# Modulation sets on VectorE: from column sweeps over a 128 x 512 accumulator to fused row sums over transposed blocks, in a hybrid encoder block

## The chip, the cores and the metric

The kernel runs on one core of a Trainium2 chip. Its time is device microseconds of one execution. A measurement is the median of several executions; for the kernel before it is 1263.94 us over three runs (1263.31 to 1264.48).

The names in the text: TensorE (PE in the profile) multiplies matrices, VectorE (DVE) does elementwise work and sums along the free dimension, ScalarE (ACT) applies functions and copies, SyncE (SP) issues the loads and stores. PEld is TensorE's loading of the stationary operand.

## The reference

One layer of an encoder block over 256 tokens of width 2048, all in float32. A conditioning vector c (2048 numbers) makes six modulation vectors of 2048 numbers each:

```
c_act = silu(c)
mod = c_act @ ada_w + ada_b                       # 2048 x 12288
shift_a, scale_a, gate_a, shift_f, scale_f, gate_f = split(mod, 6)

h = rmsnorm(x, norm1_w) * (1 + scale_a) + shift_a
proj = h @ w_in                                   # 2048 x 5184
...
x = x + gate_a * (concat(ret_out, mla_out) @ w_o)
h = rmsnorm(x, norm2_w) * (1 + scale_f) + shift_f
x = x + gate_f * ((silu(h @ w_gate) * (h @ w_up)) @ w_down)
out = rmsnorm(x, final_norm_w)
```

Between the two lines with proj and x stand eight heads of bidirectional retention and eight heads of latent attention. The change touches only how mod is computed.

## The kernel before, in words

**Layout.** Features are cut into 16 tiles of 128 (K tiles). All weights come as one stream in the order in which they are used (class Stream), in loads of mostly 128 x 1024 floats, 512 KB, into six buffers named stg. A weight tile is split into a rounded part whi (ScalarE, line 124) and a remainder wlo (VectorE, line 126), and each product takes three matmuls (lines 132 to 134): high by high, high by low, low by high. The products accumulate in eight PSUM banks.

**Stages.** The input projection runs over four groups of K tiles (GROUPS: 2, 4, 4 and 6 tiles). For each group build_h1 (line 360) makes the scaled and shifted input from xnT, the column of gain_a and the column of mod, two ScalarE operations (lines 143 and 144, tiles hfull and actt) and a VectorE subtraction (line 145) for a tile. The scale and shift of a group are therefore needed before its matmuls; they are computed during the group before. After that come retention and attention, the output projection, the second norm, the gated feed-forward and the down projection.

**Modulation sets.** mod is computed in sets (ada_set, line 174): one section (SC_A and SH_A are scale and shift of the first norm, SC_F and SH_F of the second, GT_A and GT_F the gates) and up to four feature blocks of 128, so 512 columns of ada_w. A set is either TensorE's or VectorE's, by the strings ADA_PE, ADA_PE2 and ADA_PE3. A TensorE set multiplies each weight tile by a padded copy c_pad of silu(c) (line 196) into four rows of a bank. A VectorE set has the 2048 input features on the partitions and the 512 columns along the free dimension, and sweeps the 16 K tiles:

```
V.tensor_scalar(out=a, in0=w[:, j], scalar1=c_act[:, 0:1], scalar2=None, op0=ALU.mult)
V.scalar_tensor_tensor(out=a, in0=w[:, j], scalar=c_act[:, k:k + 1], in1=a, op0=ALU.mult, op1=ALU.add)
```

(lines 198 and 200). The accumulator ada_acc then holds 128 partial sums for each column. For scale and shift, spread() turns each of the set's blocks with a TensorE transpose (line 222), sums along the free dimension (line 226, VectorE) and adds the bias (line 227). For a gate, a matmul with a matrix of ones (line 218) sums over the partitions and spreads the result to all of them at once.

Sixteen sets are VectorE's. Thirteen of them run while the pool mid is open: SH_A of blocks 2 to 5; SC_A of blocks 6 to 9, 10 to 13 and 14 to 15 (the last with 256 columns); GT_A of blocks 0, 8 and 12; SC_F of 0 and 4; SH_F of 4 and 8; and SC_F and SH_F of 12. The other three, GT_F of blocks 4, 8 and 12, run later beside the feed-forward.

**Order.** The program lists steps (the list steps, from line 370 on) and mixes the loads of the sets among the weight loads. run() issues loads up to four tiles ahead of their use. A scheduler then decides, from its own estimates, in which order each engine gets its instructions; each engine then works through its list in order, with waits on semaphores.

Of the kernel before, what the change touches and what calls it, by code (L numbers as in the profile page):

```python
# [29 lines left out]
R_GA, R_GF, R_GNW, R_GNB, R_FW, R_RD, R_FREQ = 0, 2048, 4096, 5120, 6144, 8192, 8208  # L30
N_ROWS = 8304
# [30 lines left out]
class Stream:  # L62

    def __init__(self, ap):
        self.ap, self.at, self.plan = ap, 0, []

    def take(self, name, k0, kt, c0, n):
        self.plan.append((name, k0, kt, c0, n))  # L70
        a = self.at
        self.at += P * kt * n
        return self.ap[a:self.at].rearrange("(p f) -> p f", p=P)

    def pack(self, np, weights):
        flat = np.empty(self.at, np.float32)
        a = 0
        for name, k0, kt, c0, n in self.plan:
# [7 lines left out]
def encoder_block(ctx: ExitStack, tc: tile.TileContext, x, cols, rows, pos, stream, out):  # L86
# [8 lines left out]
    def bank():  # L95
        return ps.tile([P, 512], F32, name="bank")
# [14 lines left out]
    c_act = const.tile([P, KT], F32, name="c_act")  # L111
    c_pad = const.tile([P, KT, 32], F32, name="c_pad")
# [55 lines left out]
    def f(fn, *args):  # L168
        return ("f", lambda: fn(*args), fn.__name__)
# [4 lines left out]
    def ada_set(pool, sec, k0, nk, rowdst, on_pe):  # L174
        n = nk * P
        wide = n if not on_pe else min(n, 2 * P)
# [3 lines left out]
        def acc_tile():  # L180
            return (pool or late["pool"]).tile([P, n], F32, name="ada_acc", tag="ada_acc", bufs=2 if pool else 1, padded_shape=[P, 512])

        def load(c, t):
            w = wp.tile([P, kk, wide], F32, name="stg", tag="stg", bufs=6)
            SY.dma_start(w.rearrange("p k n -> p (k n)"), stream.take("ada_w", t * kk, kk, sec * D + k0 * P + c, wide))
            return w

        def body(c, t, w):
            if c == 0 and t == 0:
                acc["t"] = bank() if on_pe else acc_tile()  # L190
            a = acc["t"]
            for j in range(kk):
                k = t * kk + j
                if on_pe:
                    q = 32 * (k % 4)
                    PE.matmul(a[q:q + 32, c:c + wide], lhsT=c_pad[:, k], rhs=w[:, j], start=c == 0 and k < 4, stop=c + wide == n and k >= KT - 4)  # L196
                elif k == 0:
                    V.tensor_scalar(out=a, in0=w[:, j], scalar1=c_act[:, 0:1], scalar2=None, op0=ALU.mult)
                else:
                    V.scalar_tensor_tensor(out=a, in0=w[:, j], scalar=c_act[:, k:k + 1], in1=a, op0=ALU.mult, op1=ALU.add)  # L200

        def finish():
            a = acc["t"]
            if on_pe:
                b, a = a, acc_tile()
                S.copy(a, b[:, 0:n])
            acc["a"] = a
            if rowdst is not None:
                r0 = (R_GA if sec == GT_A else R_GF) + k0 * P
                br = wp.tile([1, n], F32, name="bias_row", tag="stg", bufs=6)  # L210
                SY.dma_start(br, rows[:, r0:r0 + n])
                V.tensor_tensor(a[0:1, :], a[0:1, :], br, op=ALU.add)

        def spread():
            a = acc["a"]
            b = bank()
            if rowdst is not None:
                PE.matmul(b[:, 0:n], lhsT=ones, rhs=a, start=True, stop=True)
# [6 lines left out]
            parts = b[:, 0:n].rearrange("p (j q) -> p j q", q=P)  # L225
            V.tensor_reduce(out=m, in_=parts[:, :, ::32] if on_pe else parts, axis=AX.X, op=ALU.add)  # L226
            V.tensor_tensor(m, m, col[:, C_ADAB + ks.start:C_ADAB + ks.stop], op=ALU.add)
# [24 lines left out]
    mid = mid_cm.__enter__()  # L252

# [4 lines left out]
    S.activation(c_act, col[:, C_C:C_C + KT], AF.Silu)  # L258
    G.memset(c_pad, 0.0)
    V.tensor_copy(c_pad[:, :, 0:1], c_act.unsqueeze(2))  # L260
# [112 lines left out]
    steps += [f(turn_x, 0), f(build_h1, 0)]  # L373
# [51 lines left out]
    krT = mid.tile([P, T], F32, name="krT")  # L425
# [293 lines left out]
    rstd_b = mid.tile([P, T], F32, name="rstd_b")  # L719
# [273 lines left out]
```

## Time and profile before

| | |
|---|---|
| median of three runs | 1263.94 us |
| profiled execution | 1266.85 us |
| its span, first to last instruction | 1264.9 us |
| TensorE busy | 1224.4 us, 97% |
| VectorE busy | 843.6 us, 67% |
| ScalarE busy | 599.7 us, 47% |
| mean granted TensorE clock | 0.992 |
| read from memory | 312.11 MB |

The profile is one execution. Its page gives each engine's busy time, the span cut into slices, the chain of waits that ended last (from the last instruction back to what released it, step by step) and the costliest groups of instructions. Matmuls overlap, so a matmul's own duration is longer than the step from one to the next, and the step is what counts. "Idle before" is the time an engine waited ahead of an instruction, with the one that released it.

### The profile page before, as it was taken

How to read it: one execution, taken by the hardware profiler on the slowest of the kernel's cores; microseconds unless marked ns; L12 is line 12 of the kernel's file. 1: busy time of each engine (PE TensorE's matmuls, PEld its weight loads, DVE VectorE, ACT ScalarE, POOL GpSimd, SP SyncE). 2: the span in 40 equal slices, each digit the busy share in tenths (PEclk: the TensorE clock that was granted, in tenths of full speed). 3: DMA queues.
4: the chain of work that ended last, by engine and by line, in shares of the span. 5: the costliest groups of instructions: out<-in, count | busy, mean ns of one | idle time of the engine just before them, and what ended most of it. 6: DMA issues, size and time to landing. Idle time of an engine off the chain costs nothing.

```text
span 1264.9 us, 16232 instructions
## 1 busy us (share of the span) xinstructions
PE 1224.4 (97%) x6022; PEld 971.6 (77%) x6022; DVE 843.6 (67%) x1185; ACT 599.7 (47%) x811; POOL 1.7 (0%) x9
## 2 busy tenths in 40 slices
PE   5899899999999999899999999999999999999997
PEld 2676667788787788578888888888888888888885
DVE  2596988879997998886655556655654454554544
ACT  4552454645556665646344444444444434444433
POOL 0000000000000000000000000000000000000000
PEclk9999999999999999999999999999999999999998
DMA  8888898888877887897667657665765655555552
GB/s 337 321 301 309 276 317 299 290 311 290 298 255 289 306 301 278 299 349 250 211 220 233 201 183 274 222 203 202 275 219 188 226 187 194 190 198 190 192 196 88
DMA packets 88799, 315.28 MB, mean 249 GB/s; under 512 B 10248, under 2 KB 10376, under 8 KB 88208
## 3 DMA queue, kind: packets, MB, share of 16 engines
q1 hardware_dynamic: 88720, 314.24, 72.0%
q8 instruction: 47, 0.77, 0.3%
q14 instruction: 32, 0.26, 0.1%
HBM read 312.11 MB, written 2.10 MB: 248 GB/s over the span
## 4 chain that ended last, share of the span: by engine, by line
PE 85%; DVE 5%; DMA 5%; ACT 2%; issue 1%; SPq 0%; ACTq 0%; DVEq 0%
PE bank L133 25%; PE bank L134 25%; PE bank L132 25%; DMA stg<-in_stream 5%; DVE wlo L126 2%; PE bank L148 2%; PE bank L196 2%; DVE ada_acc L200 1%; ACT whi L124 1%; PE bank L514 1%; PE bank L138 1%; PE bank L513 1%; PE bank L626 1%; PE bank L615 1%; PE bank L140 1%
## 5 line engine op out<-in xcount | busy, mean ns | idle before, releaser
L126 DVE TENSOR_TENSOR wlo<-stg,whi 128x1024 fp32r<-128x1024 f32 (+2 forms) x400 | 478.7, 1198 | 341.2 <-ACT whi L124 339.6
L124 ACT CAST whi<-stg 128x1024 fp32r<-128x1024 f32 (+2 forms) x400 | 412.8, 1033 | 532.3 <-PE bank L134 417.2
L132 PE MATMUL bank<-whi,actt 128*128 128x512 f32 (+1 forms) x1184 | 457.9, 393 | 11.7 <-ACT whi L124 8.4
L133 PE MATMUL bank<-wlo,actt 128*128 128x512 f32 (+1 forms) x1184 | 461.7, 390 | 7.4 <-DVE wlo L126 7.0
L134 PE MATMUL bank<-whi,actt 128*128 128x512 f32 (+1 forms) x1184 | 459.2, 388 | 0.3 <-DVE actt L145 0.3
L132 PEld LDWEIGHTS bank<-whi,actt 128*128 128x128 f32 x1184 | 222.0, 189 | 64.9 <-ACT whi L124 12.7
L133 PEld LDWEIGHTS bank<-wlo,actt 128*128 128x128 f32 x1184 | 223.7, 189 | 62.4 <-DVE wlo L126 17.0
L134 PEld LDWEIGHTS bank<-whi,actt 128*128 128x128 f32 x1184 | 223.7, 189 | 44.9 <-DVE actt L145 1.1
L200 DVE SCALAR_TENSOR_TENSOR ada_acc<-stg,c_act,ada_acc 128x512 f32<-128x512 f32 (+1 forms) x240 | 175.0, 730 | 15.8 <-DMA stg<-in_stream 12.8
L132 PE MATMUL bank<-whi,ap 128*128 128x512 f32 x352 | 137.0, 389 | 0.0
L134 PE MATMUL bank<-whi,ap 128*128 128x512 f32 x352 | 136.9, 389 | 0.0
L133 PE MATMUL bank<-wlo,ap 128*128 128x512 f32 x352 | 136.9, 389 | 0.0
L133 PEld LDWEIGHTS bank<-wlo,ap 128*128 128x128 f32 x352 | 66.1, 188 | 13.8
L132 PEld LDWEIGHTS bank<-whi,ap 128*128 128x128 f32 x352 | 66.1, 188 | 13.8
L134 PEld LDWEIGHTS bank<-whi,ap 128*128 128x128 f32 x352 | 66.1, 188 | 13.5
L196 PE MATMUL bank<-stg,c_pad 128*32 128x256 f32 x544 | 48.0, 415 | 11.1 <-DMA stg<-in_stream 11.0
L196 PEld LDWEIGHTS bank<-stg,c_pad 128*32 128x32 f32 x544 | 13.0, 112 | 35.2 <-issue 26.0
L852 ACT ACTIVATE sgs<-bank 128x512 f32<-128x512 f32 x22 | 13.1, 597 | 10.5 <-PE bank L134 9.8
L145 DVE TENSOR_TENSOR actt<-hfull,actt 128x256 fp32r<-128x256 f32 x40 | 16.3, 420 | 2.2 <-ACT actt L144 2.1
L854 DVE TENSOR_TENSOR sgs<-bank,sgs 128x512 f32<-128x512 f32 x22 | 14.3, 682 | 0.6 <-PE bank L134 0.6
L834 DVE TENSOR_TENSOR ap<-bank,ap 128x512 fp32r<-128x512 f32 x22 | 14.1, 681 | 0.0
L226 DVE TENSOR_REDUCE mod<-bank 128x4 f32<-128x512 f32 (+3 forms) x18 | 8.0, 442 | 8.5 <-PE bank L222 8.3
(222 smaller groups left out, 711.1 us busy)
## 6 DMA issues: line engine op xcount, KB each, us to landing
stg<-in_stream SPq DMA_DIRECT2D x568, 512.0 KB, 4.4
stg<-in_stream SPq DMA_DIRECT2D x16, 288.0 KB, 4.1
stg<-in_stream SPq DMA_DIRECT2D x8, 384.0 KB, 2.8
xt<-in_x SPq DMA_DIRECT2D x2, 1024.0 KB
acc_cq<-in_x SPq DMA_DIRECT2D x8, 256.0 KB
out<-x SPq DMA_DIRECT2D x8, 256.0 KB, 2.9
acc_k<-in_rows SPq DMA_DIRECT2D x1, 1024.0 KB, 7.7
fw<-in_rows SPq DMA_DIRECT2D x1, 1024.0 KB
```

What stands on the lines that cost most here:

```text
L124: S.copy(hi, stg)
L126: V.tensor_tensor(lo, stg, hi.bitcast(F32), op=ALU.subtract)
L132: PE.matmul(o, lhsT=ah, rhs=whi, start=first, stop=False)
L133: PE.matmul(o, lhsT=ah, rhs=wlo, start=False, stop=False)
L134: PE.matmul(o, lhsT=al, rhs=whi, start=False, stop=last)
L145: V.tensor_tensor(dst[:, k, T:2 * T], tmp, dst[:, k, 0:T].bitcast(F32), op=ALU.subtract)
L148: PE.transpose(b[:, j, tb * P:(tb + 1) * P], src, ident)
L196: PE.matmul(a[q:q + 32, c:c + wide], lhsT=c_pad[:, k], rhs=w[:, j], start=c == 0 and k < 4, stop=c + wide == n and k >= KT - 4)
L200: V.scalar_tensor_tensor(out=a, in0=w[:, j], scalar=c_act[:, k:k + 1], in1=a, op0=ALU.mult, op1=ALU.add)
L834: V.tensor_tensor(ap[:, ks, T:2 * T], b, ap[:, ks, 0:T].bitcast(F32), op=ALU.subtract)
L852: S.activation(sg, o[tb], AF.Silu)
L854: V.tensor_tensor(sg, o[tb], sg, op=ALU.mult)
```

## The change: what it does

The weights of the thirteen VectorE sets in the pool mid are stored transposed in the stream: a block has 128 output features on the partitions and 1024 input features along the free dimension, again 512 KB. A new tile c_row holds silu(c) on every partition (a broadcast load of 1 MB, then silu on ScalarE). A block is one fused multiply and sum along the free dimension, whose running sum starts at the bias (first half of the input features) or at the first half's result, and which writes one column of mod. A set of four blocks has eight of them in place of sixteen sweeps over columns.

For scale and shift this leaves no transpose, no reduction and no addition of the bias. For a gate, VectorE multiplies the identity by the four columns of mod, and the matmul with ones stays. The three late GT_F sets stay as they were. TensorE sets use a 32-column window of c_act in place of c_pad, and their gate matmul uses heads4, which has ones in four rows only. The accumulator pool goes from two buffers to one, and krT and rstd_b share a buffer.

```
 class Stream:
-    def take(self, name, k0, kt, c0, n):
+    def take(self, name, k0, kt, c0, n, turned=False):
...
-            b = weights[name][k0 * P:(k0 + kt) * P, c0:c0 + n].reshape(kt, P, n).transpose(1, 0, 2)
+            b = weights[name][k0 * P:(k0 + kt) * P, c0:c0 + n]
+            b = b.T if turned else b.reshape(kt, P, n).transpose(1, 0, 2)
...
 def ada_set(pool, sec, k0, nk, rowdst, on_pe):
         n = nk * P
-        wide = n if not on_pe else min(n, 2 * P)
+        turned = not on_pe and pool is not None
+        wide = 2 * P if on_pe else P if turned else n
         kk = 1024 // wide
...
-                    PE.matmul(a[q:q + 32, c:c + wide], lhsT=c_pad[:, k], rhs=w[:, j], ...
+                    PE.matmul(a[q:q + 32, c:c + wide], lhsT=c_act[:, k:k + 32], rhs=w[:, j], ...
...
+            k = sec * KT + k0 + c // P
+            m = mod[:, k:k + 1]
+            V.tensor_tensor_reduce(
+                out=w, in0=w, in1=c_row[:, t * 1024:(t + 1) * 1024], scale=1.0, scalar=m if t else col[:, C_ADAB + k:C_ADAB + k + 1],
+                op0=ALU.mult, op1=ALU.add, accum_out=m,
+            )
...
+            elif rowdst is not None:
+                a = acc["a"] = acc_tile()
+                V.tensor_tensor(
+                    a.rearrange("p (k q) -> p k q", q=P), ident.unsqueeze(1).broadcast_to([P, nk, P]),
+                    mod[:, ks].unsqueeze(2).broadcast_to([P, nk, P]), op=ALU.mult,
+                )
...
-            for j in range(nk):
-                PE.transpose(b[:, j * P:(j + 1) * P], a[:, j * P:(j + 1) * P], ident)
...
+            if on_pe:
+                b = bank()
+                for j in range(nk):
+                    PE.transpose(b[:, j * P:(j + 1) * P], acc["a"][:, j * P:(j + 1) * P], ident)
...
+    c_row = mid.tile([P, D], F32, name="c_row")
...
+    def c_rows():
+        SY.dma_start(c_row, rows[:, R_C:R_C + D].partition_broadcast(P))
+        S.activation(c_row, c_row, AF.Silu)
+
-    steps += [f(turn_x, 0), f(build_h1, 0)]
+    steps += [f(turn_x, 0), f(build_h1, 0), f(c_rows)]
```

The scheduler's order moves with it. Three places:

ScalarE, in the first K group, after the accumulator copies of the chunk cq; before:

```order
L350 COPY acc_cq<-bank 128x512 x2
L276 COPY xnT<-bank 128x512
L124 CAST whi<-stg 128x576
L350 COPY acc_ck<-bank 128x288 x2
L276 COPY xnT<-bank 128x512
```

And with the change (lines 379, 305 and 126 are the old 350, 276 and 124):

```order
L379 COPY acc_cq<-bank 128x512 x2
L305 COPY xnT<-bank 128x512
L404 ACT_TABLE_LOAD
L404 ACTIVATE c_row<-c_row 128x2048
L126 CAST whi<-stg 128x576
L379 COPY acc_ck<-bank 128x288 x2
```

A table load and the silu of c_row stand ahead of the cast of the second 576-column tile.

VectorE, in the first of its sets (SH_A of blocks 2 to 5); before:

```order
L198 TENSOR_SCALAR ada_acc<-stg,c_act 128x512
L200 SCALAR_TENSOR_TENSOR ada_acc<-stg,c_act,ada_acc 128x512 x3
L226 TENSOR_REDUCE mod<-bank 128x4
L227 TENSOR_TENSOR mod<-mod,col 128x4
L230 SCALAR_TENSOR_TENSOR gain_a<-mod,col 128x4
L126 TENSOR_TENSOR wlo<-stg,whi 128x1024
L200 SCALAR_TENSOR_TENSOR ada_acc<-stg,c_act,ada_acc 128x512 x2
```

And with the change (line 216 is the fused sum, 128 the subtraction for wlo, 147 that of build_h1):

```order
L216 ISA stg,mod<-stg,c_row,col 128x1024
L216 ISA mod 128x1
L252 TENSOR_REDUCE mod<-bank 128x4
L216 ISA stg,mod<-stg,c_row,mod 128x1024
L216 ISA mod 128x1
L253 TENSOR_TENSOR mod<-mod,col 128x4
L256 SCALAR_TENSOR_TENSOR gain_a<-mod,col 128x4
L128 TENSOR_TENSOR wlo<-stg,whi 128x1024
L216 ISA stg,mod<-stg,c_row,col 128x1024
L216 ISA mod 128x1
L147 TENSOR_TENSOR actt<-hfull,actt 128x256
L128 TENSOR_TENSOR wlo<-stg,whi 128x1024
```

A block is two instructions, the second of one element for each partition, and the first subtraction of build_h1 for the second K group follows after the third block.

ScalarE, at the end of the first K group, where build_h1 makes the tiles of the second; before:

```order
L350 COPY acc_v<-bank 128x512 x2
L124 CAST whi<-stg 128x1024
L143 ACTIVATE hfull<-xnT,mod,gain_a 128x256
L124 CAST whi<-stg 128x1024
L350 COPY acc_g<-bank 128x512 x2
L144 ACTIVATE actt<-xnT,mod,gain_a 128x256
L143 ACTIVATE hfull<-xnT,mod,gain_a 128x256
L144 ACTIVATE actt<-xnT,mod,gain_a 128x256
```

And with the change (145 and 146 are the old 143 and 144):

```order
L379 COPY acc_g<-bank 128x512 x2
L145 ACTIVATE hfull<-xnT,mod,gain_a 128x256
L379 COPY acc_q<-bank 128x512
L126 CAST whi<-stg 128x1024
L379 COPY acc_q<-bank 128x512
L146 ACTIVATE actt<-xnT,mod,gain_a 128x256
L145 ACTIVATE hfull<-xnT,mod,gain_a 128x256
L379 COPY acc_k<-bank 128x512
L146 ACTIVATE actt<-xnT,mod,gain_a 128x256
L126 CAST whi<-stg 128x1024
L379 COPY acc_k<-bank 128x512
L126 CAST whi<-stg 128x1024
```

The pairs of hfull and actt, which stood in one run after the copies of acc_g, are spread among the copies of acc_q and acc_k, and casts of whi stand between and ahead of the copies.

## Rows read from the trace of the kernel before

**Rows 1.** The page: busy time, share of the span and instructions of each engine.

```profile
PE 1224.4 (97%) x6022; PEld 971.6 (77%) x6022; DVE 843.6 (67%) x1185; ACT 599.7 (47%) x811; POOL 1.7 (0%) x9
```

**Rows 2.** Stretches: from:to, length, busy PE, PEld, DVE, ACT, POOL, PEclk, DMA, GB/s.

```profile
25.00:75.00 50.00, 44.87 (x244) 30.91 (x243) 29.29 (x40) 30.66 (x51) 0.00 (x0) 0.96 0.83 294
75.00:240.00 165.00, 157.85 (x854) 117.50 (x853) 136.71 (x250) 71.66 (x98) 0.00 (x0) 0.99 0.89 304
240.00:510.00 270.00, 269.93 (x1544) 211.29 (x1543) 236.96 (x424) 153.43 (x273) 0.00 (x0) 1.00 0.81 287
510.00:600.00 90.00, 84.48 (x387) 65.62 (x386) 72.05 (x101) 53.59 (x75) 0.00 (x0) 0.98 0.87 308
```

**Rows 3.** Waits of TensorE, 25 to 600 us: total us, times, longest.

```profile
PE bank L132 <- ACT whi L124: 8.4, 6, 2.7
PE bank L133 <- DVE wlo L126: 7.0, 14, 1.1
PE bank L132 <- ACT actt L144: 1.3, 1, 1.3
```

**Rows 4.** Timeline of TensorE at 48 us: start, us, what, count.

```profile
47.81 0.60 PE L222 MATMUL bank<-ident,ada_acc 128*128 128x128 f32 x4
48.25 0.60 PE L148 MATMUL bank<-ident,xt 128*128 128x128 f32 x4
```

**Rows 5.** Groups of VectorE by shape: count, busy us, mean ns, idle before.

```profile
L126 DVE TENSOR_TENSOR wlo<-stg,whi 128x1024 fp32r<-128x1024 f32 x376 | 459.2, 1223 | 334.6 <-ACT whi L124 333.4
L200 DVE SCALAR_TENSOR_TENSOR ada_acc<-stg,c_act,ada_acc 128x512 f32<-128x512 f32 x225 | 167.8, 747 | 15.6 <-DMA stg<-in_stream 12.8
L200 DVE SCALAR_TENSOR_TENSOR ada_acc<-stg,c_act,ada_acc 128x256 f32<-128x256 f32 x15 | 7.2, 480 | 0.2
L198 DVE TENSOR_SCALAR ada_acc<-stg,c_act 128x512 f32<-128x512 f32 x15 | 7.2, 478 | 1.1 <-DMA stg<-in_stream 1.1
L226 DVE TENSOR_REDUCE mod<-bank 128x4 f32<-128x512 f32 x9 | 6.2, 688 | 2.4 <-PE bank L222 2.4
L227 DVE TENSOR_TENSOR mod<-mod,col 128x4 f32<-128x4 f32 x14 | 2.2, 156 | 0.1
```

**Rows 6.** The same view, groups of ScalarE.

```profile
L116 ACT ACT_TABLE_LOAD x5 | 6.4, 1283 | 0.1
L266 ACT ACTIVATE sq<-xt 128x2048 f32<-128x2048 f32 x2 | 3.8, 1910 | 3.8 <-DMA xt<-in_x 3.8
L520 ACT ACTIVATION_READ_ACCUMULATOR prob<-bank,st 128x1 f32 x16 | 3.3, 209 | 0.0
```

**Rows 7.** The chain that ended last: shares of the span by line.

```profile
by line: PE bank L133 25.0%; PE bank L134 24.8%; PE bank L132 24.6%; DMA stg<-in_stream 5.1%; DVE wlo L126 2.5%; PE bank L148 2.4%; PE bank L196 2.4%; issue 1.4%; DVE ada_acc L200 1.4%; ACT whi L124 1.3%; PE bank L514 0.8%; PE bank L138 0.7
```

**Rows 8.** Timeline of SP's queue at 18 us.

```profile
17.95 1.25 SPq L185 DMA_DIRECT2D stg<-in_stream  x2
```

**Rows 9.** DMA of the first 100 us in 40 slices of 2.5 us.

```profile
GB/s 59 328 410 410 419 415 405 413 405 402 376 44 193 362 395 398 392 138 249 351 385 331 315 375 280 257 303 292 206 246 250 302 349 351 306 346 377 320 346 285
```

**Rows 10.** Timeline of ScalarE at 30 us.

```profile
29.82 0.68 ACT L124 CAST whi<-stg 128x576 fp32r<-128x576 f32 x1
```

**Rows 11.** Timeline of TensorE at 32 us.

```profile
32.44 0.29 PE L133 MATMUL bank<-wlo,actt 128*128 128x288 f32 x1
```

**Rows 12.** Timeline of ScalarE at 71 to 74 us.

```profile
70.90 0.61 ACT L144 ACTIVATE actt<-xnT,mod,gain_a 128x256 fp32r<-128x256 f32 x1
...
73.87 0.59 ACT L144 ACTIVATE actt<-xnT,mod,gain_a 128x256 fp32r<-128x256 f32 x1
```

**Rows 13.** Timeline of TensorE at 71 us; in brackets the idle time before.

```profile
71.56 0.50 PE L132 MATMUL bank<-whi,actt 128*128 128x512 f32 x1 [1.32 <-ACT actt L144]
```

**Rows 14.** Waits of ScalarE, 25 to 240 us.

```profile
ACT whi L124 <- DMA stg<-in_stream: 49.4, 23, 4.9
```

**Rows 15.** Stretches, line 200 alone: length, DVE busy, PEclk, DMA, GB/s.

```profile
240.00:510.00 270.00, 66.77 (x90) 1.00 0.81 287
```

More of the change, by code (lines that the diff above doesn't have):

```diff
@@ L180, in acc_tile @@
         def acc_tile():
-            return (pool or late["pool"]).tile([P, n], F32, name="ada_acc", tag="ada_acc", bufs=2 if pool else 1, padded_shape=[P, 512])
+            return (pool or late["pool"]).tile([P, n], F32, name="ada_acc", tag="ada_acc", bufs=1, padded_shape=[P, 512])
         def load(c, t):
-            w = wp.tile([P, kk, wide], F32, name="stg", tag="stg", bufs=6)
-            SY.dma_start(w.rearrange("p k n -> p (k n)"), stream.take("ada_w", t * kk, kk, sec * D + k0 * P + c, wide))
+            w = wp.tile([P, 1024], F32, name="stg", tag="stg", bufs=6)
@@ L186, in load @@
+            SY.dma_start(w, stream.take("ada_w", t * kk, kk, sec * D + k0 * P + c, wide, turned))
             return w
         def body(c, t, w):
[L189 to L193, printed above, removed]
-                if on_pe:
[L195 to L207, printed above, removed]
-            if rowdst is not None:
[L209 to L218, printed above, removed]
+            if on_pe:
+                w = w.rearrange("p (k n) -> p k n", k=kk)
+                if c == 0 and t == 0:
+                    acc["t"] = bank()
+                a = acc["t"]
+                for j in range(kk):
+                    k = t * kk + j
+                    q = 32 * (k % 4)
+                    PE.matmul(a[q:q + 32, c:c + wide], lhsT=c_act[:, k:k + 32], rhs=w[:, j], start=c == 0 and k < 4, stop=c + wide == n and k >= KT - 4)
+                return
@@ new lines, in body @@
+            if not turned:
+                if t == 0:
+                    acc["t"] = acc_tile()
+                a = acc["t"]
+                for j in range(kk):
+                    k = t * kk + j
+                    wj = w[:, j * n:(j + 1) * n]
+                    if k == 0:
+                        V.tensor_scalar(out=a, in0=wj, scalar1=c_act[:, 0:1], scalar2=None, op0=ALU.mult)
+                    else:
+                        V.scalar_tensor_tensor(out=a, in0=wj, scalar=c_act[:, k:k + 1], in1=a, op0=ALU.mult, op1=ALU.add)
+                return
@@ new lines, in body, with finish @@
+            k = sec * KT + k0 + c // P
[4 more added lines that the diff above has]
+            )
+        def finish():
+            ks = slice(sec * KT + k0, sec * KT + k0 + nk)
+            if not turned:
+                a = acc["a"] = acc_tile() if on_pe else acc["t"]
+                if on_pe:
+                    S.copy(a, acc["t"][:, 0:n])
+                if rowdst is not None:
+                    r0 = (R_GA if sec == GT_A else R_GF) + k0 * P
+                    br = wp.tile([1, n], F32, name="bias_row", tag="stg", bufs=6)
+                    SY.dma_start(br, rows[:, r0:r0 + n])
+                    V.tensor_tensor(a[0:1, :], a[0:1, :], br, op=ALU.add)
+            elif rowdst is not None:
[4 more added lines that the diff above has]
+                )
@@ L424, in encoder_block @@
     krd = mid.tile([P, NB, 2, 64], F32, name="krd")
-    krT = mid.tile([P, T], F32, name="krT")
+    krT = mid.tile([P, T], F32, name="krT", tag="krT")
     def kr_rope():
@@ L717, in turn_x2 @@
             S.copy(x2T[k // 8][:, k % 8:k % 8 + 2], b)
-    rstd_b = mid.tile([P, T], F32, name="rstd_b")
+    rstd_b = mid.tile([P, T], F32, name="rstd_b", tag="krT")
     def norm_x2():
```

32 lines of the change are left out of this document (19 added, 13 removed).

## The prediction

> **What bounds the kernel now.** I read the page first. TensorE is busy for 97% of the span and VectorE for 67% [rows 1]; that average hides stages, so next I cut the span into stretches [rows 2]. The reader is to see four. From 25 to 75 us TensorE idles 5.1 us of 50. From 75 to 240 us it idles 7.2 us of 165, while VectorE is busy for 83% and the DMA engines for 89%. From 240 to 510 us it is never idle: 269.93 us of 270. From 510 to 600 us it idles 5.5 us. So up to 600 us TensorE, VectorE and the DMA stand close to each other, and the middle stretch belongs to TensorE alone. Then I asked what TensorE waited for between 25 and 600 us [rows 3]: 8.4 us for whi from ScalarE, 7.0 us for wlo from VectorE, 1.3 us for the scaled activations. These 17 us are all that a faster VectorE or a better order can give back; the rest must come out of TensorE's own work.
>
> **The change part by part.** The sum is made against the profiled execution, which took 1266.85 us, 1.95 us more than its span; the median of the runs shown is 1263.94 us, 2.9 us less. I add the changes to the median.
>
> *TensorE work removed.* Of the 13 VectorE sets that change, 10 are shift or scale sets (nine of four blocks, one of two), and each of their 38 blocks loses its transpose. Four such transposes start at 47.81 us and the next matmul at 48.25 us [rows 4]: 0.44 us, or 0.11 us each. 38 x 0.11 = 4.2 us. Sixteen of the 38 (sets SC_F 0 and 4, SH_F 4 and 8) belong to the stretch where TensorE never idles, 1.8 us; the other 22 stand where TensorE is busy for 90% or more, so I take them whole: **-4.2 us**. The three gate_a sets keep their one matmul, with a product of ident and mod in place of the accumulated sum.
>
> *VectorE's sets.* Before, a set of 512 columns is one multiply of 478 ns and 15 fused steps of 747 ns, 11.7 us, and the set of 256 columns is 16 steps of at most 480 ns, 7.7 us [rows 5]: 12 x 11.7 + 7.7 = 148 us. After, these sets are 100 blocks, each a fused multiply-and-sum over 1024 elements and, as the order shows, a second small instruction that delivers the sum. Neither is in this trace. The first is bounded from below by the two-input subtract of the same size, 1223 ns [rows 5]; from above by two fused steps of 512, 1494 ns, which read the same data. I take 1.22 us, since the subtract has the same two SBUF inputs and size, and a running sum inside the engine adds no input. The second lies between VectorE's smallest operation, 156 ns [rows 5], and ScalarE's accumulator read, 209 ns [rows 6]; I take 0.18 us. A block is then 1.40 us against 1.48 us for two steps: 140 us against 148 us. The ten reductions go too, 9 x 0.69 + 0.4 us, with ten additions of 0.16 us: 8 us. So VectorE has some 16 us less of its 843.6 us. Little of that is on the path: line 200 has 1.4% of the chain of waits [rows 7], 17.7 us of its 175 us, a tenth. A tenth of 16 us is 1.6 us: **-1.5 us**, between nothing and all 7.0 us of waiting for wlo.
>
> *The broadcast row: its load.* The 1 MB of c_row is issued on SP's queue between the two loads that go out from 17.95 us on [rows 8], and every later load moves behind it. At the 400 GB/s of that time it takes 2.6 us. But the DMA engines then fall idle, 44 and 193 GB/s in the slices from 27.5 to 32.5 us [rows 9], because all six stg buffers are full: that hole swallows it. **0**, at worst +2.6 us if a load is late.
>
> *The broadcast row: silu on ScalarE.* The order puts a table load and the silu of 2048 elements ahead of the cast of the second 576-column tile. Priced by the first table load, 1283 ns, and the 2048-element square, 1910 ns [rows 6], that is 3.2 us. The cast begins at 29.82 us now [rows 10], so after at 33.0 us; wlo follows 0.7 + 0.8 us later, at 34.5 us, and TensorE wants it at 32.44 us [rows 11]: **+2 us**, between nothing (if the matmuls before are late anyway) and 3.2 us. c_row itself should be there: issued near 18.5 us, it needs its own 2.6 us and at most six 0.5 MB loads ahead, 7.7 us at 400 GB/s, so it lands by 29 us, before ScalarE asks for it at 29.9 us. That is close.
>
> *Order on ScalarE before the second K group.* A column of mod is now complete after two blocks instead of after a whole set, so the scheduler spreads the four pairs of hfull and actt over the preceding copies, and casts of whi move ahead of copies. Now they come in one run from 70.90 us to 74.4 us [rows 12], with TensorE waiting 1.32 us for the first [rows 13] and ScalarE's casts behind it. I take **-2 us**, between nothing and the 1.3 us plus the longest whi wait, 2.7 us [rows 3].
>
> The padded copy of silu(c), the smaller accumulator pool and the shared buffer of krT and rstd_b cost nothing: the first stood under the first load's wait, the accumulators are emptied before the next set ends, and krT is last read long before rstd_b is written. Three 2 KB bias loads go; SP waits for buffers, not for issue.
>
> Sum: -4.2 - 1.5 + 0 + 2 - 2 = -5.7 us; 1263.9 - 5.7 = **1258.2 us**. With every term at its good end, -4.2 - 7.0 - 4.0 = -15 us; at its bad end, -4.2 + 2.6 + 3.2 = +1.6 us.
>
> **Rivals.** *The gain stays hidden.* For: in 75 to 240 us the DMA engines are 89% busy and ScalarE waited 49.4 us for stg in 25 to 240 us [rows 2, 14], so a quicker VectorE only waits sooner. Then only the 16 transposes of the full stretch count, and the silu costs its 2 us: 1263.9 - 1.8 + 2 = 1264 us. Against: TensorE idles only 7.2 us there, so its own work still counts.
>
> *ScalarE is held in the first K groups (slower).* The spread hfull pairs now stand in its in-order queue ahead of accumulator copies and whi casts, and each waits for a column of mod, so for two blocks and their loads. Waits for stg average 49.4/23 = 2.1 us [rows 14]. If each of the four pairs holds the queue that long, 8.6 us come in place of the -2 us: 1263.9 - 3.7 + 8.6 = 1268.8 us. It decides once those holds together pass 3.7 us. For: TensorE has no other work queued there than the matmuls behind those casts. Against: the order has the blocks well ahead of the pairs.
>
> *The fused sum runs at half rate (much slower).* From 256 to 512 columns a fused step grows by 267 ns, 1.04 ns an element [rows 5]; a second such step per element adds 1.07 us to a block, 107 us in all. Between 240 and 510 us line 200 has 90 of its steps [rows 15], six sets, so 48 blocks would add 51 us, where VectorE idles 33 us [rows 2]: at least 18 us late there, 1264 - 4 + 18 = 1278 us or more. It decides once a block passes about 1.6 us. Against: the fused step already reads two f32 inputs from SBUF and pays 1.04 ns an element.
>
> [...]
>
> **How the numbers follow.** Forecast 0.55; hidden gain 0.22; ScalarE held 0.16; half rate 0.07. A measurement of this kernel tells about 0.2%, 2.5 us, from no change, so the forecast counts as faster, the hidden gain as the same, the last two as slower: 0.55, 0.22, 0.23. The range runs from 1250 us (most of the good end) to 1269 us, which takes in the held ScalarE and leaves out the half rate.
>
> **What would show it.** Right: blocks of 1.2 to 1.3 us plus 0.15 to 0.2 us on VectorE; ada_acc transposes 26 in place of 64; a TensorE gap near 32 us of about 2 us and none near 71 us; VectorE's busy time near 828 us; 240 to 510 us shorter by about 1.8 us. Wrong: blocks above 1.6 us; ScalarE idle before hfull on mod; c_row landing after 30 us; more TensorE idle than 17.9 us from 25 to 600 us.

## The result and the profile after

The changed kernel takes 1269.74 us, the median of 6 runs (1268.35 to 1273.71), beside 1263.38 us for the kernel before (6 runs, 1261.45 to 1264.48): a ratio of 1.0055, 95% interval 1.0039 to 1.0071. It is slower by some 6 us where 5.7 us faster was forecast. A second series beside later experiments gave 1.0037, interval 1.0024 to 1.0050.

VectorE's work fell, and 38 of TensorE's transposes are gone. The first fence is the page's busy time, which answers to [rows 1]; its second line is the same for a second trace of the kernel before (e16 below). The next fence has the groups by shape, where [rows 5] has lines 200 and 226.

```profile
PE 1220.2 (96%) x5984; PEld 968.2 (76%) x5984; DVE 821.8 (65%) x1156; ACT 600.2 (47%) x811; POOL 2.4 (0%) x14
PE 1219.4 (97%) x6022; PEld 968.7 (77%) x6022; DVE 843.5 (67%) x1185; ACT 599.6 (48%) x811; POOL 1.7 (0%) x9
```

```profile
L216 DVE CUSTOM_DVE_ANT_0 stg<-stg,c_row,col 128x1024 f32<-128x1024 f32 x50 | 64.0, 1279 | 3.6 <-DMA stg<-in_stream 3.6
L216 DVE CUSTOM_DVE_ANT_0 stg<-stg,c_row,mod 128x1024 f32<-128x1024 f32 x50 | 63.8, 1277 | 2.0 <-DMA stg<-in_stream 1.8
...
L216 DVE DVE_READ_ACCUMULATOR2_ANT mod<- 128x1 f32 x100 | 8.2, 82 | 0.0
...
L250 PE MATMUL bank<-ident,ada_acc 128*128 128x128 f32 x26 | 4.6, 290 | 0.6 <-ACT ada_acc L226 0.6
```

VectorE is busy for 21.8 us less, and a block costs 1.28 us plus 0.08 us. TensorE is busy for 4.2 us less than in the first trace of the kernel before, but its two traces, with the same instructions, differ by 5.0 us, so this number doesn't price the transposes. Yet the span is longer: TensorE waits more and, as shown below, runs slower for a while after some waits. The stretches (length, then busy PE, PEld, DVE, ACT, POOL, PEclk, DMA, GB/s) stand against [rows 2], the waits of TensorE from 25 to 600 us against [rows 3].

```profile
25.00:75.00 50.00, 42.50 (x233) 29.46 (x232) 25.45 (x37) 33.46 (x52) 0.00 (x0) 0.97 0.86 307
75.00:240.00 165.00, 154.69 (x812) 114.71 (x811) 129.78 (x232) 66.44 (x89) 0.00 (x0) 0.98 0.87 304
240.00:510.00 270.00, 268.90 (x1517) 209.80 (x1516) 226.70 (x419) 154.58 (x274) 0.00 (x0) 1.00 0.83 287
510.00:600.00 90.00, 86.03 (x417) 67.31 (x416) 70.42 (x100) 53.96 (x77) 0.00 (x0) 0.98 0.84 309
```

```profile
PE bank L134 <- ACT whi L126: 11.1, 7, 2.7
PE bank L135 <- DVE wlo L128: 9.3, 13, 1.4
PE bank L150 <- DVE rout L349: 1.1, 1, 1.1
```

TensorE is idle for 2.4 us more in the first stretch and 3.2 us more in the second, and waits for split weights 20.4 us instead of 15.4.

Two places are visible. First, ScalarE from 28 to 33 us, and TensorE's idle moments there (in brackets: idle before, and what ended it):

```profile
28.64 1.28 ACT L404 ACT_TABLE_LOAD   x1
29.93 1.91 ACT L404 ACTIVATE c_row<-c_row 128x2048 f32<-128x2048 f32 x1
31.75 0.66 ACT L126 CAST whi<-stg 128x576 fp32r<-128x576 f32 x1
```

```profile
32.46 0.53 PE L134 MATMUL bank<-whi,actt 128*128 128x288 f32 x2 [1.14 <-ACT whi L126]
37.87 0.73 PE L134 MATMUL bank<-whi,actt 128*128 128x512 f32 x2 [1.62 <-ACT whi L126]
```

The cast that began at 29.82 us [rows 10] begins at 31.75 us, and TensorE waits for a cast twice. Second, VectorE at 212 us:

```profile
210.91 1.28 DVE L381 TENSOR_TENSOR acc_g<-acc_g,bank 128x512 f32<-128x512 f32 x2
212.11 0.45 DVE L325 TENSOR_SCALAR ang<-freq,posf 128x96 f32<-128x96 f32 x2
...
216.56 0.33 DVE L335 TENSOR_SCALAR sc_t<-ang 128x96 f32<-128x96 f32 x2
216.80 1.89 DVE L128 TENSOR_TENSOR wlo<-stg,whi 128x1024 fp32r<-128x1024 f32 x2
```

These are the rotary tables: 32 small operations in one piece of 4.7 us, with two weight tiles' subtracts behind them. The change doesn't touch their code. Before, the scheduler had spread them between the fused steps of line 200, from the 39th to the 44th weight tile, in the third K group. Some of the kernel before:

```profile
152.72 0.74 DVE L200 SCALAR_TENSOR_TENSOR ada_acc<-stg,c_act,ada_acc 128x512 f32<-128x512 f32 x1
153.39 0.20 DVE L299 TENSOR_SCALAR turns<-turns 128x96 f32<-128x96 f32 x1
153.51 0.75 DVE L200 SCALAR_TENSOR_TENSOR ada_acc<-stg,c_act,ada_acc 128x512 f32<-128x512 f32 x1
```

With those steps gone it leaves them together behind the 57th tile, at the start of the fourth group. ScalarE's timeline shows what follows; the last line, for comparison, is the kernel before:

```profile
216.33 0.67 ACT L126 CAST whi<-stg 128x576 fp32r<-128x576 f32 x1 [2.04 <-DVE turns L333]
...
235.42 0.20 ACT L118 ACTIVATE stat<-stat 128x2 f32<-128x2 f32 x1 [0.16 <-DVE stat L117]
243.58 0.47 ACT L145 ACTIVATE hfull<-bank,col 128x256 f32<-128x256 f32 x1 [7.95 <-PE bank L150]
...
238.73 0.47 ACT L143 ACTIVATE hfull<-bank,col 128x256 f32<-128x256 f32 x1 [2.71 <-PE bank L148]
```

A cast waits 2.0 us for the tables, and the latents come late: ScalarE idles 7.95 us ahead of their first scaling instead of 2.71 us.

To see where each kernel falls behind, I take the start of the same matmul (the n-th with wlo) in each trace, less its start in the first trace of the kernel before. All in us.

| at, in the kernel before | 30.5 | 45.4 | 64.5 | 74.6 | 95.8 | 143.5 | 165.4 | 209.4 | 256.8 | 501.5 | 576.4 |
|---|---|---|---|---|---|---|---|---|---|---|---|
| before, second trace | -1.1 | -1.1 | -1.7 | -1.7 | -1.7 | -1.7 | -4.5 | -4.7 | -5.5 | -4.8 | -6.2 |
| the change | -1.3 | +3.9 | +3.0 | +0.9 | +2.7 | +2.2 | -1.6 | -1.2 | +4.6 | +5.1 | +1.5 |
| the change, second trace | -1.5 | +3.6 | +2.7 | +0.6 | +2.9 | +2.4 | -1.4 | -0.9 | +4.4 | +5.0 | +1.5 |
| before + row (e1) | +1.3 | +6.5 | +6.3 | +6.4 | +6.1 | +5.7 | +4.9 | +5.2 | +5.9 | +5.9 | +5.8 |
| change, row early (e3) | +0.5 | +0.5 | +0.4 | -1.7 | +0.1 | -0.3 | -3.8 | -3.3 | +2.6 | +4.8 | +1.9 |
| change, tables back (e5) | +1.7 | +5.2 | +4.4 | +2.2 | +4.1 | +3.6 | +4.4 | +3.5 | +1.7 | +2.5 | -1.0 |
| change, both (e6) | +0.3 | +0.3 | +0.2 | -1.9 | -0.1 | -0.5 | +0.9 | -0.1 | -2.5 | -2.5 | -5.3 |
| change, both, second (e15) | +0.2 | +0.2 | +0.1 | -2.0 | -0.3 | -0.7 | +0.4 | -0.7 | -3.1 | -3.0 | -6.5 |
| before, tables late (e7) | -1.5 | -1.5 | -1.3 | -1.3 | -0.5 | -0.9 | -4.4 | -3.1 | +2.3 | +3.2 | +3.2 |

The first row warns: two executions of the same unchanged kernel, 1266.85 and some 1260.6 us, differ by 6 us, in steps at a few places. The two traces of the change are the lowest of their series. So a step counts below only where every trace with a feature has it and every trace without it lacks it, and totals are taken from the ratios.

A part of the steps is the granted clock, which the profile gives for each stretch. In the places looked at here it falls to 0.5 of full speed for 3.4 or 6.8 us at a time, right behind waits of TensorE. Here are 30 to 46 us of the change and of the change with the tables back (e5), then 209 to 262 us of the change and of the kernel before (columns as in [rows 2]; PEclk is the third number from the end):

```profile
30.00:46.00 16.00, 13.24 (x83) 8.80 (x80) 3.12 (x3) 8.67 (x14) 0.00 (x0) 0.89 0.82 306
30.00:46.00 16.00, 13.24 (x103) 8.86 (x98) 3.12 (x3) 10.79 (x16) 0.00 (x0) 1.00 0.80 266
209.00:262.00 53.00, 48.05 (x288) 38.29 (x286) 44.89 (x115) 28.32 (x52) 0.00 (x0) 0.94 0.78 260
209.00:262.00 53.00, 51.56 (x332) 41.20 (x331) 42.85 (x88) 28.98 (x52) 0.00 (x0) 1.00 0.85 293
```

The first two have the same waits of 1.14 and 1.62 us. Behind the second one the clock fell for 3.4 us in the change and stayed at full in e5.

### The profile page after: what moved, and what is told of

Same layout as the page of the kernel before. It is cut to its first block, busy times and chain, and to the rows that moved or that the text cites. A ratio compares the mean times of both kernels' runs of the same rounds, so it can differ in the third digit from the quotient of the medians.

```text
span 1266.3 us, 16085 instructions
## 1 busy us (share of the span) xinstructions
PE 1220.2 (96%) x5984; PEld 968.2 (76%) x5984; DVE 821.8 (65%) x1156; ACT 600.2 (47%) x811; POOL 2.4 (0%) x14
## 4 chain that ended last, share of the span: by engine, by line
PE 86%; DVE 5%; DMA 4%; ACT 2%; issue 2%; SPq 0%; ACTq 0%; DVEq 0%
PE bank L135 26%; PE bank L136 25%; PE bank L134 25%; DMA stg<-in_stream 4%; PE bank L200 3%; PE bank L150 2%; DVE wlo L128 2%; DVE stg L216 1%; ACT whi L126 1%; PE bank L547 1%; PE bank L546 1%; PE bank L659 1%; PE bank L648 1%; PE bank L571 1%; PE bank L140 0%
## 5 line engine op out<-in xcount | busy, mean ns | idle before, releaser
L216 DVE CUSTOM_DVE_ANT_0 stg<-stg,c_row,col 128x1024 f32<-128x1024 f32 x50 | 64.0, 1279 | 3.6 <-DMA stg<-in_stream 3.6
L216 DVE CUSTOM_DVE_ANT_0 stg<-stg,c_row,mod 128x1024 f32<-128x1024 f32 x50 | 63.8, 1277 | 2.0 <-DMA stg<-in_stream 1.8
L200 PE MATMUL bank<-stg,c_act 128*32 128x256 f32 x544 | 48.9, 416 | 11.9 <-DMA stg<-in_stream 11.8
L212 DVE SCALAR_TENSOR_TENSOR ada_acc<-stg,c_act,ada_acc 128x512 f32<-128x512 f32 x45 | 33.8, 751 | 10.6 <-DMA stg<-in_stream 9.7
L200 PEld LDWEIGHTS bank<-stg,c_act 128*32 128x32 f32 x544 | 13.0, 112 | 36.0 <-issue 27.0
```

The source lines that it names most:

```text
L200: PE.matmul(a[q:q + 32, c:c + wide], lhsT=c_act[:, k:k + 32], rhs=w[:, j], start=c == 0 and k < 4, stop=c + wide == n and k >= KT - 4)
L212: V.scalar_tensor_tensor(out=a, in0=wj, scalar=c_act[:, k:k + 1], in1=a, op0=ALU.mult, op1=ALU.add)
L216: V.tensor_tensor_reduce(out=w, in0=w, in1=c_row[:, t * 1024:(t + 1) * 1024], scale=1.0, scalar=m if t else col[:, C_ADAB + k:C_ADAB + k + 1],
```

## The experiments

**The row (e1, e11, e3).** Load and silu of c_row were added to the kernel before, unused, at the change's place; then the load alone; then the changed kernel made the row at the start from c_act.

```diff
 # e1 (before); e11 is the same without the silu
...
+    def c_rows():
+        c_row = big.tile([P, D], F32, name="c_row", tag="m8")
+        SY.dma_start(c_row, rows[:, R_C:R_C + D].partition_broadcast(P))
+        S.activation(c_row, c_row, AF.Silu)
...
+    steps += [f(turn_x, 0), f(build_h1, 0), f(c_rows)]
```

```diff
 # e3 (the change)
-        SY.dma_start(c_row, rows[:, R_C:R_C + D].partition_broadcast(P))
-        S.activation(c_row, c_row, AF.Silu)
...
+        V.tensor_tensor(dg, ident.unsqueeze(1)..., c_act[:, 0:KT].unsqueeze(2)..., op=ALU.mult)
+        for n in range(4):
...
+            PE.matmul(b, lhsT=ones, rhs=dg[:, 4 * n:4 * n + 4], start=True, stop=True)
+            V.tensor_copy(c_row[:, n * CH:(n + 1) * CH], b)
...
+    steps = [f(c_rows), f(norm_x)]
```

> The kernel before with the row of silu(c) loaded and activated at the place where the change does it, and used by nothing. Theory: the table load and the silu of 3.2 us ahead of the cast of the second 576-column tile hold TensorE for about 3 us in the first K group and nothing gives it back, so about 1266.4 us, 3 us over the kernel before. Rival (the fused blocks themselves, or waits for single columns of mod, make the change slow): the row is hidden, 1263.4 us.

Measured: 1270.05 us, ratio 1.0041 (1.0024 to 1.0059), some 5 us.

> The kernel before with the row's load of 1 MB (unused), without the silu on ScalarE. Theory (the loss of the run with load and silu, 5 us, is the silu in ScalarE's queue ahead of a weight tile's cast): 1264 to 1266 us. Rival (it is the load, which holds back weight loads behind it): 1268 to 1270 us.

Measured: 1267.23 us, ratio 1.0013 (1.0001 to 1.0025), some 1.6 us. So by the medians most of e1's loss comes with the silu. The 1.6 us are not the price of the load alone, for the order moved too: the second 576-column tile is cast 4 us later than in [rows 10], behind two copies of acc_ck and one more of xnT that stand after the cast in the kernel before:

```profile
31.86 0.79 ACT L350 COPY acc_ck<-bank 128x288 f32<-128x288 f32 x2 [0.60 <-PE bank L134]
33.41 0.59 ACT L276 COPY xnT<-bank 128x512 f32<-128x512 f32 x1 [0.76 <-PE bank L148]
33.89 0.67 ACT L124 CAST whi<-stg 128x576 fp32r<-128x576 f32 x1
```

> The change with the row made at the start by VectorE (identity times silu(c)), four matmuls with ones and four copies on VectorE, while TensorE waits for its first loads; no broadcast load and no silu in the first K group. Theory (the row's place costs 3 us): about 1266.7 us. Rival (blocks or waits for mod): 1269.7 us as with the change.

Measured: 1267.71 us, ratio 1.0016 (1.0003 to 1.0030), 3 to 5 us below the change by the ratios. From 30.5 to 45.4 us TensorE falls back by 5.2, 5.1, 5.1 and 3.6 us in the four traces of the table with the silu, and by 0.0 in every trace without row load. The 3.6 us are e5's, where the clock stayed at full.

**The place of the rotary tables (e5, e7).** In the change the tables' step was listed inside the third K group; in the mirror, the kernel before got one tiny operation that ties the tables to the last result of that group.

```diff
 # e5 (the change)
+            if gi == 2 and i == 4:
+                steps.append(f(rotary_tables))
...
-        if gi == 2:
-            steps.append(f(rotary_tables))
```

```diff
 # e7 (before), in rotary_tables
         V.tensor_copy(posf, post)
+        V.scalar_tensor_tensor(out=posf, in0=pacc["g"][:, 0, 1022:1024], scalar=0.0, in1=posf, op0=ALU.mult, op1=ALU.add)
```

> The change with the step that makes the rotary tables listed earlier, so that VectorE does it after its 40th subtraction for wlo, as in the kernel before, and not after its 57th, as in the change; nothing else is edited. Theory (the scheduler moved 5 us of small VectorE operations into the start of the fourth K group, where TensorE then waits for wlo, and took them out of the third): about 4 us less than the change, 1265.7 us. Rival (blocks, waits for mod or the row alone): 1269.7 us, since the same work only stands elsewhere.

Measured: 1265.54 us, ratio 1.0003 (0.9988 to 1.0018): with the tables listed earlier, the change costs nothing measurable.

> The kernel before with one tiny operation that makes the rotary tables depend on the last result of the third K group, so that they run in one piece after the 57th weight tile as in the change; nothing else of the change. Theory (the place of the tables costs 5 us): 1269 to 1271 us against 1264.9. Rival (VectorE has room there too, what the other kernel gained by moving them back was something else): 1264 to 1266 us.

Measured: 1271.18 us, ratio 1.0055 (1.0038 to 1.0073). The kernel before with nothing but the tables' place changed is as slow as the change. Its VectorE shows the same piece, and the three fences after it the waits of TensorE from 215 to 262 us, of this kernel, of the change and of the change with both side effects out (e15):

```profile
210.78 0.44 DVE L297 TENSOR_SCALAR ang<-freq,posf 128x96 f32<-128x96 f32 x2
...
215.22 0.33 DVE L307 TENSOR_SCALAR sc_t<-ang 128x96 f32<-128x96 f32 x2
215.46 1.89 DVE L126 TENSOR_TENSOR wlo<-stg,whi 128x1024 fp32r<-128x1024 f32 x2
```

```profile
PE bank L132 <- ACT whi L124: 2.3, 1, 2.3
PE bank L133 <- DVE wlo L126: 2.2, 2, 1.6
```

```profile
PE bank L135 <- DVE wlo L128: 2.5, 2, 1.4
PE bank L134 <- ACT whi L126: 2.5, 1, 2.5
```

```profile
PE bank L135 <- DVE wlo L128: 0.4, 1, 0.4
```

From 209.4 to 256.8 us TensorE falls back by 5.3 to 5.9 us in all four traces of the table with the tables at the start of the fourth K group, and moves ahead or stays (+0.7 at most) in all others. In those four TensorE is idle for 4.5 to 5.0 us there, 1.4 us in the first trace of the kernel before, and behind the waits, from 231 to 233 us on, the granted clock fell to 0.5 for 3.4 us (e7) or 6.8 us (the others); in no other trace of the table did it fall in this stretch.

**Both out, and each kernel again (e6, e15, e8, e16).** e6 and e15 are one kernel: the change with e3's row and e5's place of the tables.

> The change with both side effects taken out: the row of silu(c) made at the start from c_act (as in the run with the early row) and the rotary tables listed in the third K group (as in the run with them put back). Theory (two separate losses, each from one place, and a gain of the sets beneath them): the ratios add, 1.0055 - 0.0039 - 0.0052 = 0.9964, about 1260.4 us against 1264.9 us of before. Rival (time lost early is caught up at the next wait for weights, or the sets give nothing): no better than the kernel with the rotary tables put back alone, 1264.5 to 1266 us.

> The change with both side effects taken out (row early, tables back in the third K group) again, beside the kernel before on the same chip, for a second trace of each. Theory (the sets are worth some 6 us after 50 us, as the first trace shows): 1258 to 1261 us, ratio 0.995 to 0.998. Rival (1 us, as the first twelve runs show): 1262.5 to 1264.5 us, ratio 0.998 to 1.0.

Measured: 1263.47 us, ratio 0.9991 (0.9979 to 1.0004), then 1262.55 us, 0.9986 (0.9975 to 0.9997). So 1 to 2 us are gained in all, where the forecast had 7.7 for sets and order (its 4.2, 1.5 and 2). Taken out alone, the row and the tables give 3.0 and 4.3 thousandths (from 1.0046, the mean of the two series of the change), together 5.7; whether the two losses add is within the noise of the four ratios.

But the tables are not back where they were. In e5, e6 and e15 VectorE makes them in one piece again, behind the 40th weight tile, and not spread from the 39th to the 44th. From e15, the first and last of VectorE's piece, and TensorE's wait from 143 to 166 us:

```profile
149.23 0.44 DVE L325 TENSOR_SCALAR ang<-freq,posf 128x96 f32<-128x96 f32 x2
...
153.66 0.33 DVE L335 TENSOR_SCALAR sc_t<-ang 128x96 f32<-128x96 f32 x2
```

```profile
PE bank L135 <- DVE wlo L128: 3.1, 2, 2.6
```

Between 143.5 and 165.4 us these three fall back by 0.8 to 1.4 us, while the four traces with the later tables move ahead by 3.4 to 3.8 us. Measured against those four, the tables cost some 4 to 5 us here, and some 4 and 1 us in the two traces of the kernel before (0.0 and -2.8 in the same stretch). So the 1 to 2 us are not the sets alone.

> The change itself, beside the others on the same chip, for a second trace of it. Theory: 1.0055 of before, 1270 to 1272 us, and in the trace the same two steps: TensorE 4 to 5 us later after the row's silu and 5 to 6 us later after the rotary tables. Rival (the steps of the first trace belong to that one execution): no such steps.

> The kernel before against itself, for a second trace: ratio 1.000 within 0.0015 if the comparison is fair. Theory (the first trace, of an execution 2 us above the median, is late in one place): its later twin is 2 us earlier from that place on. Rival (executions differ everywhere a little): the offset grows steadily.

Measured: the change again 1269.28 us, 1.0037 (1.0024 to 1.0050), with both steps in the table as before; the kernel before against itself 1.0000 (0.9984 to 1.0016). Its second trace is 6 us shorter than the first. The largest step, 2.8 us, lies between 143 and 165 us, where the tables stand: the first trace has a wait of 2.56 us there and, behind it, 3.4 us at a granted clock of 0.5; the second has waits of 0.54 us at most and the full clock. The stretch in the first trace, in the second, and in e15:

```profile
143.00:166.00 23.00, 19.27 (x109) 14.24 (x108) 18.48 (x48) 6.36 (x7) 0.00 (x0) 0.93 0.88 296
143.00:166.00 23.00, 20.90 (x130) 13.87 (x130) 21.74 (x60) 9.97 (x11) 0.00 (x0) 1.00 0.92 330
143.00:166.00 23.00, 19.03 (x98) 13.92 (x98) 18.89 (x54) 7.50 (x8) 0.00 (x0) 0.85 0.85 300
```

**The transposes alone (e2).** The kernel before without the 38 transposes; the sum then runs over the accumulator's own columns, so the sum over partitions is left out.

```diff
-            b = bank()
+            b = bank() if on_pe or rowdst is not None else a
...
-            for j in range(nk):
-                PE.transpose(b[:, j * P:(j + 1) * P], a[:, j * P:(j + 1) * P], ident)
+            if on_pe:
+                for j in range(nk):
+                    PE.transpose(b[:, j * P:(j + 1) * P], a[:, j * P:(j + 1) * P], ident)
```

> The kernel before without the transposes of its VectorE shift and scale sets: the reduction reads the accumulator itself, so the sum over partitions is left out. This prices the term of TensorE work removed. As predicted, 38 transposes of 0.11 us: 4.2 us less, 1259.2 us. Rival (the gain stays hidden): only the 16 in the stretch from 240 to 510 us count, 1261.6 us, or none, 1263.4 us.

Measured: 1265.55 us, ratio 1.0012 (0.9998 to 1.0027): no gain. In its trace TensorE is 5.3 us ahead of the first trace of the kernel before at 257 us and has lost all of it by 457 us. The waits there, of TensorE and of ScalarE:

```profile
456.24 0.74 PE L132 MATMUL bank<-whi,actt 128*128 128x512 f32 x1 [2.85 <-ACT whi L124]
```

```profile
455.14 1.04 ACT L124 CAST whi<-stg 128x1024 fp32r<-128x1024 f32 x1 [3.18 <-DMA stg<-in_stream]
```

TensorE meets a weight tile that is not there yet, and the granted clock falls to 0.5 for 3.4 us behind the wait. That being ahead is the reason isn't shown: the second trace of the kernel before is as far ahead at 257 us (-5.5) and loses nothing at 457. This run also moved the decay tables to a later tile, so it is not the transposes alone; why the tile is late stays open.

**Single columns of mod (e4).** The blocks wrote to a second table, copied into mod at a set's end.

```diff
+    modt = const.tile([P, 6 * KT], F32, name="modt")
...
-            m = mod[:, k:k + 1]
+            m = modt[:, k:k + 1]
...
+            if turned:
+                V.tensor_copy(mod[:, ks], modt[:, ks])
```

> The change with the fused blocks writing to a second table, and one copy into the modulation table at a set's end, so that ScalarE's hfull can only follow a whole set, as before the change; the row and the rotary tables stay where the change has them. Theory (ScalarE's 4.1 us of waits on single columns are covered): 1269 to 1271.5 us, like the change. Rival (ScalarE held by hfull is the loss): 1264 to 1267 us.

Measured: 1269.75 us, ratio 1.0048 (1.0028 to 1.0068), like the change. In the change ScalarE does wait for single columns (its waits from 25 to 240 us). In e4 these are gone, and the time is the same:

```profile
ACT hfull L145 <- DVE mod L216: 4.1, 3, 1.6
```

**The tables out of everyone's way (e9, e17, e10, e12, e13, e14).** The tables' operations go to the start, behind the norm of x (e9 and e17 with the change and the early row, one kernel; e10 with the kernel before), or ahead of it with their inputs loaded before x (e12, e13); e14 is e12 with the row's diagonal ahead of the tables.

```diff
 # e9, against e3
...
+    def rotary_sin():
         S.activation(sc_t, sc_t, AF.Sin)
...
-    steps = [f(c_rows), f(norm_x)]
+    steps = [f(c_rows), f(norm_x), f(rotary_tables)]
...
         if gi == 2:
+            steps.append(f(rotary_sin))
```

> The change with the row of silu(c) made at the start from c_act, and the rotary tables computed at the start of the program, right behind the norm of x, where VectorE has little to do. Theory (each piece of small VectorE work costs where it stands in front of weight tiles; offsets of TensorE between the traces show 3.5 to 3.8 us for the tables in the third K group and 6 us in the fourth): 3 to 4 us less than the kernel with both side effects taken out (1263.5), 1259.5 to 1261 us, faster than both kernels. Rival (the tables and the Sin table load now delay the first weight tiles instead): 1264 to 1267 us.

> The fastest kernel so far (row at the start, tables behind the norm of x) again: theory 1259 to 1261.5 us, ratio 0.995 to 0.998; rival (its nine runs were lucky): 1262.5 to 1264.5 us.

Measured: 1260.19 us, ratio 0.9962 (0.9946 to 0.9979); again 1260.82 us, 0.9970 (0.9958 to 0.9983). **This version beats both kernels**, by 4 to 5 us against before and some 10 against the change by the ratios.

> The kernel before with the rotary tables computed at the start of the program, nothing of the change. Theory: 3 to 4 us less than before, 1260.5 to 1262 us against 1264.7. Rival (the start is delayed, or the gain is lost at the next wait for weights): 1264 to 1267 us. Beside the run above it tells what the turned blocks are worth once the tables are out of the way in both: theory 1 to 2 us, rival (nothing) 0.

Measured: 1267.07 us, ratio 1.0020 (1.0006 to 1.0034): slower. The kernel before doesn't gain from the same move.

> As the run with row and tables at the start, but the tables' inputs are loaded ahead of x and the tables computed in the stretch in which VectorE waits for ScalarE's squares (5 to 11 us), ahead of the norm of x instead of behind it, where they had put the first matmul of the projections 4.5 us later. Theory (the tables are free in that stretch): 3 to 4 us less than that run's 1260.2, 1256 to 1258 us. Rival (the 4.5 us were caught up at a later wait anyway): 1259.5 to 1261 us.

> The kernel before with the tables in that same stretch, nothing of the change. Theory: 2.8 us less than the kernel before with the tables behind the norm of x (1267.1), 1263 to 1265 us; the difference to the run beside it is then what the turned blocks and the early row are worth where the tables stand in neither's way: 6 to 8 us, near the 5.7 us of the prediction's sum. Rival (the 7 us between the earlier pair came from how their starts differ, the turned blocks are worth 1 to 2 us): 3 us or less between the two.

Measured: 1264.53 us, 1.0003 (0.9993 to 1.0013), and 1266.47 us, 1.0010 (0.9996 to 1.0024). For e12 neither theory held; for the pair the rival did, 1 to 2 us between the two. In e12 the tables' inputs hold x back, so ScalarE's first square waits 4.73 us, against 3.60 us in e9, and TensorE makes the row only behind the tables; the first projection matmul is 5.2 us late. ScalarE and TensorE of e12, then TensorE of e9:

```profile
7.76 1.91 ACT L299 ACTIVATE sq<-xt 128x2048 f32<-128x2048 f32 x1 [4.73 <-DMA xt<-in_x]
```

```profile
12.21 6.57 PE L406 MATMUL bank<-cdiag,ones 128*128 128x512 f32 x8 [12.21 <-DVE cdiag L403]
```

```profile
5.32 6.53 PE L406 MATMUL bank<-cdiag,ones 128*128 128x512 f32 x8 [5.32 <-DVE cdiag L403]
```

> As the run with row and tables in the stretch of the squares, with the row's diagonal made first and the tables behind it, so that neither the row's matmuls nor the Sin stand ahead of the first sets (there the row's matmuls ended at 18.8 us instead of 11 and the first matmul of the projections came 5.2 us late). Theory (what is late at the start stays late to the end): the first matmul 1 to 2 us late, and the time 3 to 4 us below that run's 1264.5, 1260 to 1262 us. Rival (the start is caught up by 75 us): 1264 to 1266 us.

Measured: 1261.39 us, ratio 0.9969 (0.9956 to 0.9981): repairing the start (first projection matmul 1.9 us late) gives back some 3 to 4 us, and no more than e9 has. Against e13, with the tables in the same stretch, it is 4.1 thousandths less, some 5 us, the early row included.

## Why the prediction was wrong

- **The step that failed first was one that isn't in it.** The sum priced the sets, the row and ScalarE's order at two places, and put the rest of the order at nothing without a reason. The rotary tables moved by 18 weight tiles; they are not among the three places of the order looked at. Their place costs some 7 us on its own (e7), and with them listed earlier the change is no slower than the kernel before (e5). They are 4.7 us of small operations, but in one piece ahead of weight tiles' subtracts. TensorE waits 3.0 to 3.5 us longer there, and the rest of the 5.3 to 5.9 us stands beside the fall of its granted clock to 0.5 behind these waits.
- **The row: "0" for the load and "+2" for the silu; the two together cost some 5 us** (e1, interval 3.0 to 7.5; the load alone 1.6 us, in another order, e11). The mechanism was the one forecast: silu in ScalarE's queue ahead of the second 576-column cast. That wait is 1.14 us. What the step missed is the second wait, 1.62 us for the next tile's cast at 37.87 us, and the granted clock behind it: TensorE falls back by 5.1 to 5.2 us where the clock fell and by 3.6 us where it didn't. Whether the hole in the DMA [rows 9] swallowed the load isn't shown, since e11 also moved the cast.
- **TensorE's "-4.2": the price of a transpose holds, the sum doesn't.** The 16 transposes of the stretch where TensorE never idles stand between 372 and 489 us. From one matmul with wlo to the same one, three of their four sets save 0.42 to 0.46 us, 0.11 us each as forecast. The fourth saves 0.04 us, and the new order takes 0.8 us back between 398 and 412 us, where eight matmuls of a TensorE set in one run (405.48 to 406.05 us before, 0.57 us) became two and six (from 408.04 and 411.08 us in the change, 0.55 and 0.56 us). From 360 to 501.5 us that leaves 0.6 us, forecast 1.8: 141.1 us in the change, e5, e6 and e15 against 141.7 us in both traces of the kernel before, e1 and e7. No run isolates the other 22.
- **ScalarE's order, "-2": right and then lost.** The table has -2.1 us between 64.5 and 74.6 us in every kernel in which hfull follows single columns, and between 0.0 and +0.2 us where it doesn't. By 95.8 us 1.8 to 2.3 us of it are given back, and e4, without it, is no slower. Ahead of a stretch in which the DMA is 96% busy the gain bought nothing.
- **VectorE's block was slightly overpriced:** 1.40 us forecast, 1.36 us as the sum of the two instructions; VectorE's 21.8 us less against 16 forecast. What that is worth on the path, forecast -1.5 us, no run isolates. The half-rate rival is out: a block's main instruction takes 1278 ns, where that rival put 1.07 us on top of 1.22. Its threshold of 1.6 us a block doesn't follow from its rows either: 33 us of idle VectorE over 48 blocks allow some 0.7 us more than the 1.4 us, 2.1 us. A block reads two f32 SBUF inputs of 1024 elements and delivers an accumulated sum, and its 1278 ns, beside 1223 ns of the two-input subtract of the same size [rows 5], show no halved rate.
- **The slower rival had nearly the right time (1268.8 us) for the wrong reason.** ScalarE's waits on mod are there, 4.1 us, but e4 takes them out and changes nothing. Of the forecast's signs of being wrong, this wait and the idle time of TensorE from 25 to 600 us (22.9 us, threshold 17.9) came; blocks above 1.6 us and a late c_row did not.

Open: what the sets are worth by themselves. e6 and e15 show 1 to 2 us, with the tables in one piece in the third K group. Between e10 and e9, with the tables at the start of both, it is 5.8 thousandths, 7 us; between e13 and e14 5 us; between e13 and e12, whose start is late, 1 us; the early row is included in all three. Added up from the parts, the change's 1.0046 less e1's 4.1 and e7's 5.5 thousandths leaves a gain of 5.0 thousandths, some 6 us: an estimate that takes the parts to add. So the forecast's gain for the sets may have been near, and the row and the tables, +2 and nothing in the forecast, some 5 and 7 us in the runs, turned it. The two executions of the kernel before, 6 us apart, show how much such waits swing without any change.

## What to carry to other kernels

When an edit removes fillers from an engine's order, look in the new order for what had been spread between them: a piece of small operations that closes up ahead of the bound engine's next input can cost more than the edit saves (here 4.7 us of them cost some 7 us, e7). Price an instruction put ahead of a weight's cast by the second tile behind it too (here waits of 1.14 us for the first and 1.62 us for the second), and move such preparation to a stretch where nobody waits for its engine. Look at the granted clock behind each wait of TensorE: where it fell here, the wait cost more than its own length (those two waits put TensorE back by 5.1 to 5.2 us with the fall, by 3.6 us without it). A few microseconds between two profiled executions are no evidence until a second trace of the unchanged kernel lacks them; and a run that takes a side effect out must be looked at too, since here it put the tables back in the group but not in their old places.

## What the runs showed of the hardware

The accumulator read that follows each fused block took 82 ns, about half of the smallest operation in [rows 5], 156 ns, with no idle time ahead of it. In e12 Sin needed no table load of its own behind silu: it stands behind the squares, the only load ahead of it is silu's at 0.74 us, and the next, 1.28 us, comes for the square root behind it.

```profile
12.31 0.52 ACT L338 ACTIVATE sc_t<-sc_t 128x384 f32<-128x384 f32 x1
12.86 1.28 ACT L118 ACT_TABLE_LOAD   x1
```
